# Causal attention that takes the query roots in its softmax's scale, and memory queries loaded in two halves of tokens

## The chip, the core and the metric

The kernel runs on one core of a Trainium2 chip. The metric is the device time of one execution in microseconds; three executions of the kernel before took 2182.63, 2183.37 and 2185.61 us, so the median is 2183.37.

In the profile the engines are PE (TensorE, matmuls and transposes), PEld (its weight loads), DVE (VectorE), ACT (ScalarE), POOL (GpSimd) and SP (SyncE, which issues all the loads and stores here). Each engine works its own instructions in order and waits on semaphores for the others.

## What is computed

One layer of a decoder trunk on 1024 tokens of width 1024 in float32: a half-step SwiGLU, a mixer with three gated branches, and another half-step SwiGLU. The change lies in the mixer. Cut to what matters:

```python
h = rmsnorm(x, mix_norm);  z = h @ w_in        # u | v | c_q | c_kv | k_rope | q_mem | gates
y_a = u * (tril(W_s) @ layernorm(v) + b)       # chunks of 128 tokens, 8 groups of 64
q = rmsnorm(q_up, q_norm)                      # c_q up to 8 heads of 96 (64 plain, 32 rotary)
q = concat(q[..., :64], rope(q[..., 64:]))     # k the same way, its rotary part shared
s = where(causal, (q @ k.T) * 96**-0.5, -1e30)
y_b = softmax(s) @ v                           # 8 heads, 1024 tokens
y_c = memory_attention(q_mem, mem)             # 4 heads of 128, 256 memory tokens
x = x + (sum_i sigmoid(gate_i) * (y_i @ W_branch_i)) @ W_out
```

The root of a query's RMSNorm is one number per token and head. A rotation works within a token and head, so such a factor may be applied before it, after it, or on the scores.

## The kernel before

**Products.** Float32 values are held as two parts, hi and lo, and a product is three matmuls, hi by hi, hi by lo, lo by hi (`mm3`, L156 to L163, matmuls at L160 to L162). `split` (L135 to L139) makes the parts: a cast on ACT (L136) and a difference on DVE (L139). `split_gain` (L151 to L154) does it with a gain per partition. PSUM gives two "mm" buffers of two banks each and four single "bank" buffers. A matmul row of 512 columns whose output is a bank, with operands named x and whi or wlo, is a branch product in the stretch that matters here.

**What sets the order.** A scheduler orders the instructions of each engine, from the order of the code and its own costs; `after(i, first)` (L414) holds an instruction behind another one of its engine. `self.hold` does so for every ACT cast of `split`, and for weight loads. SP issues all loads in its own order over eight rotating semaphores, so no more than eight transfers are in flight.

**qkv** (L440 to L503) works on pairs of token tiles, four passes. Queries and keys go up from their latents, ACT copies them out and squares them, DVE sums the squares, and an iterated reciprocal root gives r, 16 numbers per token tile pair and partition for q and 16 for k. DVE multiplies all of q by its roots (L490, 128x1536), POOL rotates q's rotary part (L369 to L374), DVE multiplies k (L492). The results go to DRAM: v (L478), k (`kd`, L495), q (`qd`, L498). The memory key and value weights (wkv, L808) are loaded in the same stretch.

**sgu** (L569 to L620) is the gated branch, in two halves of 512 tokens: `split(hf)` makes the parts of v, `mix(hf)` mixes tokens with eight group matrices, evicts with a bias on ACT (L591), transposes (L597), multiplies by u (loaded at L594), and splits. Between the halves lies `mem_kv` (L777 to L799), the memory's keys (split with a gain, L152 and L153) and values. Behind it the memory's queries are loaded (`mem_queries`, L814 to L822, issue L820): per head a hi and a lo tile of 128 features x 1024 tokens, 512 KB each. Heads 0 and 1 go to tiles named h, heads 2 and 3 to the tiles v_hi and v_lo of the first half, and those are issued first.

**Memory attention** (L824 to L881) follows a list written out by hand of S (scores of 128 tokens, 4 heads against 256 memory tokens, one mm buffer), T (transposes), V (values) and F. F is one step of branch a's output product, which fills PE in between; it loads a gate (L521) and multiplies on DVE (L1045). A score's chain is: DVE reduce (L838), DVE product with the roots of the memory queries (L839), four exps on ACT (L843, their scale one column of the negated roots), reciprocal (L847), normalisation on POOL (L848). The exps read the mm buffer, so the buffer is free when the fourth is done.

**Causal attention** (L889 to L1036) works head by head on pairs j of token tiles 2j and 2j+1, 32 steps. `prepare` transposes q and k of the next head and splits them with their gains. `scores` makes the scores of two tiles, one mm buffer each. For each, DVE adds the mask, writes the result to a tile pr and takes the minimum (L946; the gain has a minus sign, so the minimum is the maximum of the scores); ACT then takes the exps with that column as bias, scale -1, and a running sum (L952). `turn` transposes the exps in blocks (L968) into banks and splits them, `value` multiplies them with v (L983, L984) and evicts (L991, L992). The loop runs the turn one step and the value two steps behind the scores.

Of the kernel before, what the change touches and what calls it, by code (L numbers as in the profile page):

```python
# [8 lines left out]
F32 = mybir.dt.float32  # L9
# [3 lines left out]
ACT = mybir.ActivationFunctionType  # L13
# [3 lines left out]
P = 128  # L17
D = 1024
S = 1024
# [30 lines left out]
class Kernel:  # L50
# [84 lines left out]
    def split(self, hi, lo, src, eng=None):  # L135
        i = self.nc.scalar.copy(hi, src)  # L136
        if self.hold is not None:
            self.after(i, self.hold)
        return (eng or self.nc.vector).tensor_tensor(lo, src, hi.bitcast(F32), op=ALU.subtract)  # L139

    def split_after(self, hi, lo, src):
        i = self.nc.scalar.copy(hi, src)
        self.nc.vector.tensor_tensor(lo, src, hi.bitcast(F32), op=ALU.subtract)
        return i
# [294 lines left out]
    def qkv(self, lat, asides):  # L439
# [8 lines left out]
        with tc.tile_pool(name="qkvp", bufs=1) as p, tc.tile_pool(name="q1", bufs=1) as p1:  # L448
            for i0 in range(0, NT, 2):
                k = p.tile([P, T, H, QK], F32, name="k", bufs=2)  # L450
                q = (p1 if i0 % 4 else p).tile([P, T, H, QK], F32, name="q")
# [36 lines left out]
                bq = r[:, 0].unsqueeze(3)  # L488
                bk = r[:, 1].unsqueeze(3)
                nc.vector.tensor_tensor(q, q, bq.to_broadcast([P, T, H, QK]), op=ALU.mult)  # L490
                self.rotate(nc.gpsimd, q[:, :, :, NOPE:], q[:, :, :, NOPE:], tabs, [P, T, H, half])
                mark = nc.vector.tensor_tensor(k, k, bk.to_broadcast([P, T, H, QK]), op=ALU.mult)  # L492
                for t in range(T):
                    d = self.kd[:, :, i0 + t].rearrange("g p e -> p g e")
                    nc.sync.dma_start(d, k[:, t].rearrange("p (g x) d -> p g (x d)", x=2))  # L495
                for t in range(T):
                    d = self.qd[:, :, i0 + t].rearrange("g p e -> p g e")
                    self.queue = nc.sync.dma_start(d, q[:, t].rearrange("p (g x) d -> p g (x d)", x=2))  # L498
# [4 lines left out]
    def branches(self, br, yt, sink):  # L503

        nc, a, w = self.nc, self.a, {}

        steps = [(dt, hf) for hf in range(2) for dt in range(3)]
        steps += [(dt, hf) for dt in range(3, DT) for hf in range(2)]

        def weights(d):  # L510
            if d not in w:
                x = self.load(a["w_branch"][br, d // 2])
                w[d // 2 * 2], w[d // 2 * 2 + 1] = x[:4], x[4:]

        weights(0)
        yield
        for n, (dt, hf) in enumerate(steps):
            for d, _ in steps[n:n + 2]:
                weights(d)
            sig = self.row()  # L520
            nc.sync.dma_start(sig, self.sig[br * DT + dt][:, hf])  # L521
# [48 lines left out]
    def sgu(self, rows, p, sink):  # L570
        nc, a, tc = self.nc, self.a, self.tc
        v8 = lambda tag, hf, dt=F32R: (p if hf else self.pv).tile([P, 4, SGW], dt, name=tag)
        if True:
# [8 lines left out]
            def mix(hf):  # L582
# [4 lines left out]
                for g in range(SGG):  # L587
                    b = self.bank()[:, :4 * SGW // SGG].rearrange("p (c d) -> p c d", c=4)
                    cols = slice(g * SGW // SGG, (g + 1) * SGW // SGG)
                    self.mm3(b, w[g], tuple(x[:, :, cols] for x in v), True, True)  # L590
                    nc.scalar.activation(views[g // 4][:, :, g % 4], b, ACT.Identity, bias=self.sg_b[:, g:g + 1])  # L591
                for j in range(4):
# [6 lines left out]
                    i = self.split_after(*(t[:, hf * 512:hf * 512 + 512] for t in yt[j]), u)  # L599
                return i, z  # L600
# [8 lines left out]
            split(1)  # L609
            nc.scalar.activation(self.stat("warm", 1), vs[1][0][:, 3, SGW - 1:].bitcast(F32), ACT.Exp, scale=0.0)  # L610
# [4 lines left out]
            late = self.mem_queries(1, iter([tuple(x[:, i] for x in rooms) for i in range(2)]), z)  # L615
            queries = self.mem_queries(0, iter(lambda: self.split_pair(self.h4), None), z) + late
# [197 lines left out]
    def mem_queries(self, pair, rooms, first):  # L814

        out = []
        for o in range(2):
            qs = next(rooms)
            for t, src in zip(qs, self.mq[2 * pair + o]):
                self.after(self.nc.sync.dma_start(t.bitcast(F32), src), first)  # L820
            out.append(qs)
        return out  # L822

    def mem_attention(self, qt, rooms, kt, vv, filler):  # L824
# [5 lines left out]
        def scores(i, k):  # L830
            t = 2 * i + k
            sc = self.mm().rearrange("p a (b m) -> p (a b) m", b=2)
            for hh in range(MH):
                self.mm3(
                    sc[:, hh], tuple(x[:, t * P:(t + 1) * P] for x in qt[hh]), tuple(x[:, hh] for x in kt),
                    True, True)
            mx = self.stat("m_mx", MH)
# [34 lines left out]
        F = lambda: next(filler, None)  # L872
        yt = [self.split_pair(self.h4) for _ in range(MH)]
        for f, *x in (
                (F,), (F,), (S, 0, 0), (F,), (S, 0, 1), (F,), (F,), (T, 0, 0), (S, 1, 0), (F,), (T, 0, 1), (S, 1, 1),
# [13 lines left out]
    def attention(self):  # L889
# [15 lines left out]
        with tc.tile_pool(name="att", bufs=1) as p:  # L905
# [21 lines left out]
            def scores(h, j):  # L927
# [7 lines left out]
                for t in range(2):  # L935
# [14 lines left out]
                    prs.append(pr)  # L950
                for t, (pr, n) in enumerate(zip(prs, ns)):
                    nc.scalar.activation(  # L952
                        pr[:, :n], pr[:, :n], ACT.Exp, bias=mx[:, t:t + 1], scale=-1.0, accum_out=rs[:, t:t + 1])
# [1263 lines left out]
```

## Time and profile before

The profiled execution took 2181.75 us by the device; its span in the trace is 2180.0 us.

| What | Value |
|---|---|
| median of three runs | 2183.37 us |
| profiled execution, its span | 2181.75 us, 2180.0 us |
| mean granted TensorE clock | 0.999 |
| instructions | 27531 |
| read from and written to HBM | 229.33 MB, 109.84 MB |
| first loads of wkv behind qkv's third pass, issued | 1103.74 us |
| memory attention, first score | 1154.00 us |
| causal attention | about 1267 to 1410 us |

Times within the trace count from the span's start. A row of the timeline has the start, the time, the engine, the line of the code, the operation, output and inputs by the program's names with partitions x elements, and in brackets how long the engine had been idle before and who released it. A row of the waits has the total, the number of times and the longest. A row of the windows has the stretch and its length, busy time and (instructions) of PE, PEld, DVE, ACT and POOL, the granted clock, the busy share of the DMA engines and GB/s. A row of a line's view has the number of instructions, least, median and greatest nanoseconds, and the first and last start; a row of the groups has the number, the busy time in us and the mean in ns. A matmul of 512 columns is shown with 0.39 us but the next one starts 0.23 us later, since they are pipelined; one of 256 columns follows after 0.12.

### The profile page before, as it was taken

Reading aid. Unit: us, or ns where it says so; the run is one execution under the profiler, and the core shown is the slowest. Engines: PE = TensorE matmul, PEld = TensorE weight load, DVE = VectorE, ACT = ScalarE, POOL = GpSimd, SP = SyncE. Lnnn points to the kernel's source line nnn. Section 1 sums busy time; section 2 is a strip of 40 time slices with the busy share of each in tenths; the row PEclk is TensorE's granted clock in tenths of the full one; section 3 lists DMA queues with packets and bytes.
Section 4 is the critical chain, followed back from the end, with each engine's and each line's share of the span. In section 5 each row is a group of like instructions: output and inputs, shape, how many; then the busy total and the mean of one; then the engine's idle time right before and its main releaser. Section 6 shows DMA issues by size and latency. Waiting matters only on the chain.

```text
span 2180.0 us, 27531 instructions
## 1 busy us (share of the span) xinstructions
PE 2160.0 (99%) x10154; PEld 1802.9 (83%) x10154; DVE 1574.5 (72%) x2374; ACT 911.4 (42%) x1491; POOL 273.5 (13%) x278
## 2 busy tenths in 40 slices
PE   9999999999999999999999999999999999999999
PEld 5888888888887888888988889988888888888887
DVE  7976666679889656655895679885886666657884
ACT  5433333343445334433554368833432222224332
POOL 2011111100000000000232321140011211210000
PEclk9999999999999999999999999999999999999999
DMA  4264554385433444541685731093043233337443
GB/s 146 92 218 163 185 176 174 137 319 172 130 116 104 147 166 166 209 147 61 231 320 217 266 121 59 30 351 123 34 140 102 93 101 99 114 130 291 169 130 106
DMA packets 128823, 340.98 MB, mean 156 GB/s; under 512 B 15152, under 2 KB 23472, under 8 KB 128688
## 3 DMA queue, kind: packets, MB, share of 16 engines
q1 hardware_dynamic: 128688, 339.22, 44.5%
q8 instruction: 80, 1.31, 0.2%
q14 instruction: 55, 0.45, 0.1%
HBM read 229.33 MB, written 109.84 MB: 156 GB/s over the span
## 4 chain that ended last, share of the span: by engine, by line
PE 91%; DVE 5%; ACT 2%; issue 1%; DMA 1%; POOL 0%; SPq 0%; ACTq 0%; DVEq 0%; POOLq 0%
PE one L160 15%; PE one L161 15%; PE one L162 15%; PE bank L160 12%; PE bank L162 12%; PE bank L161 12%; PE mm L160 2%; PE mm L161 2%; PE mm L162 2%; PE bank L968 1%; PE bank L983 1%; PE bank L984 1%; PE bank L432 1%; DVE wlo L149 1%; DVE wlo L139 0%
## 5 line engine op out<-in xcount | busy, mean ns | idle before, releaser
L148 ACT CAST whi<-x 128x1024 fp32r<-128x1024 f32 (+1 forms) x203 | 193.2, 955 | 419.4 <-PE one L161 141.7
L149 DVE TENSOR_TENSOR wlo<-x,whi 128x1024 fp32r<-128x1024 f32 (+1 forms) x203 | 242.2, 1194 | 57.9 <-ACT whi L148 21.6
L1376 DVE TENSOR_TENSOR t<-t,one 128x512 f32<-128x512 f32 x188 | 129.0, 686 | 194.0 <-PE one L162 193.8
L160 PE MATMUL bank<-h,whi 128*128 128x512 f32 x636 | 247.6, 390 | 0.0
L162 PE MATMUL bank<-h,wlo 128*128 128x512 f32 x636 | 247.5, 389 | 0.0
L161 PE MATMUL bank<-h,whi 128*128 128x512 f32 x636 | 247.5, 389 | 0.0
L160 PE MATMUL one<-h,whi 128*128 128x512 f32 x516 | 202.3, 392 | 0.0
L161 PE MATMUL one<-h,whi 128*128 128x512 f32 x516 | 201.5, 391 | 0.0
L162 PE MATMUL one<-h,wlo 128*128 128x512 f32 x516 | 201.3, 390 | 0.0
L160 PE MATMUL one<-w,whi 128*128 128x512 f32 x432 | 168.6, 390 | 0.0
L162 PE MATMUL one<-w,wlo 128*128 128x512 f32 x432 | 168.1, 389 | 0.0
L161 PE MATMUL one<-w,whi 128*128 128x512 f32 x432 | 168.1, 389 | 0.0
L139 DVE TENSOR_TENSOR wlo<-w,whi 128x1024 fp32r<-128x1024 f32 (+2 forms) x112 | 114.7, 1038 | 70.1 <-ACT whi L136 69.9
L136 ACT CAST whi<-w 128x1024 fp32r<-128x1024 f32 (+2 forms) x112 | 99.0, 901 | 149.8 <-PE bank L161 53.7
L1958 POOL TENSOR_TENSOR raw<-raw 128x512 f32<-128x512 f32 x38 | 56.9, 1498 | 783.6 <-DVE raw L1813 684.8
L162 PEld LDWEIGHTS bank<-h,wlo 128*128 128x128 f32 x636 | 119.4, 188 | 24.9
L161 PEld LDWEIGHTS bank<-h,whi 128*128 128x128 f32 x636 | 119.4, 188 | 24.7
L160 PEld LDWEIGHTS bank<-h,whi 128*128 128x128 f32 x636 | 119.4, 188 | 24.6
L160 PE MATMUL bank<-whi 128*128 128x512 f32 x352 | 136.9, 389 | 0.0
L161 PE MATMUL bank<-wlo,whi 128*128 128x512 f32 x352 | 136.9, 389 | 0.0
L162 PE MATMUL bank<-whi,wlo 128*128 128x512 f32 x352 | 136.9, 389 | 0.0
L162 PEld LDWEIGHTS one<-h,wlo 128*128 128x128 f32 x516 | 97.3, 189 | 20.3
(391 smaller groups left out, 4913.2 us busy)
## 6 DMA issues: line engine op xcount, KB each, us to landing
x<-in_ffn_w_gu_dram SPq DMA_DIRECT2D x78, 512.0 KB, 4.9
w<-tdt SPq DMA_DIRECT2D x40, 512.0 KB, 4.5
gate<-raw SPq DMA_DIRECT2D x33, 512.0 KB, 2.9
tdb<-raw SPq DMA_DIRECT2D x64, 256.0 KB, 2.2
h<-in_ffn_w_down_dram SPq DMA_DIRECT2D x64, 256.0 KB, 6.0
w<-tdb SPq DMA_DIRECT2D x30, 512.0 KB, 4.4
tdt<-w SPq DMA_DIRECT2D x48, 256.0 KB, 2.3
x<-in_w_gate_dram SPq DMA_DIRECT2D x22, 512.0 KB, 7.1
```

Of the source, the lines that this page charges most:

```text
L136: i = self.nc.scalar.copy(hi, src)
L139: return (eng or self.nc.vector).tensor_tensor(lo, src, hi.bitcast(F32), op=ALU.subtract)
L148: self.nc.scalar.copy(hi, src)
L149: return lambda: self.nc.vector.tensor_tensor(lo, src, hi.bitcast(F32), op=ALU.subtract)
L160: i = mmul(out, s[0], m[0], start=first, stop=False, **kw)
L161: mmul(out, s[0], m[1], start=False, stop=False, **kw)
L162: self.last = mmul(out, s[1], m[0], start=False, stop=last, **kw)
L432: nc.tensor.transpose(b[:m, k * P:(k + 1) * P], s, self.ident)
L968: nc.tensor.transpose(b[:, at:at + P], prs[t][:, kk * P:(kk + 1) * P], self.ident)
L983: nc.tensor.matmul(o, w, pt[0], start=n == 0, stop=False)
L1376: return self.nc.vector.tensor_tensor(out, x, y, op=ALU.add)
L1958: sub = lambda d, x, y: (eng or nc.gpsimd).tensor_tensor(d, x, y, op=ALU.subtract)
```

## The change

1. In `qkv` the multiply of q by its roots goes (L490). POOL keeps the negated roots in a table `q_nr` (128 x 8 tiles x 8 heads), and q is rotated and written unscaled. Of the tile pools, q gets the two buffers that k had, and k takes q's arrangement. `self.queue`, behind which weight loads are held, is now the k write and no longer the q write.
2. In the causal attention a new DVE instruction per pair multiplies the two minima by -1 and the roots, and the exps take the root's column as scale. Both exps of a pair read that instruction's result.
3. `mem_queries` loads 512 tokens of all four heads per call, 256 KB a load, 16 loads. The first halves are held behind the last load of u as before; the second halves behind the gate load `sig_mark`, at a place Q in the list. Heads 0 and 1 are tiles named h as before, and are now issued in the order of the heads' list.
4. The first matmul of S(0,0) and S(0,1) is held behind the product before it (`after(first, last)`).
5. In `sgu` the split of v's second half runs inside `mix(0)`, held behind its last L591. The casts of branch a's weights are held behind the last cast of `mem_kv`.

```diff
     def split(self, hi, lo, src, eng=None):
-        i = self.nc.scalar.copy(hi, src)
+        self.cast = i = self.nc.scalar.copy(hi, src)
...
-                bq = r[:, 0].unsqueeze(3)
+                nc.gpsimd.tensor_scalar(self.q_nr[:, i0:i0 + T], r[:, 0], -1.0, None, op0=ALU.mult)
                 bk = r[:, 1].unsqueeze(3)
-                nc.vector.tensor_tensor(q, q, bq.to_broadcast([P, T, H, QK]), op=ALU.mult)
                 self.rotate(nc.gpsimd, q[:, :, :, NOPE:], q[:, :, :, NOPE:], tabs, [P, T, H, half])
...
+                if then:
+                    self.hold = i
+                    then()
+                    self.hold = None
...
-            mark, _ = mix(0)
-            kv = next(kv)
-            _, z = mix(1)
+            mix(0, second)
+            kv, mark = next(kv), self.cast
+            z = mix(1)
...
+    def mem_queries(self, qs, half, first):
+
+        c = slice(half * 512, half * 512 + 512)
+        for ts, src in zip(qs, self.mq):
+            for t, x in zip(ts, src):
+                self.after(self.nc.sync.dma_start(t[:, c].bitcast(F32), x[:, c]), first)
...
+                last = self.last
+                first = self.mm3(
                     sc[:, hh], tuple(x[:, t * P:(t + 1) * P] for x in qt[hh]), tuple(x[:, hh] for x in kt),
                     True, True)
+                if i == hh == 0:
+                    self.after(first, last)
...
-                (F,), (F,), (S, 0, 0), (F,), (S, 0, 1), (F,), (F,), (T, 0, 0), (S, 1, 0), (F,), (T, 0, 1), (S, 1, 1),
+                (F,), (F,), (Q,), (S, 0, 0), (F,), (S, 0, 1), (F,), (F,), (T, 0, 0), (S, 1, 0), (F,), (T, 0, 1), (S, 1, 1),
...
+                nr = self.q_nr[:, 2 * j:2 * j + 2, h]
+                nc.vector.scalar_tensor_tensor(mx, in0=mx, scalar=-1.0, in1=nr, op0=ALU.mult, op1=ALU.mult)
                 for t, (pr, n) in enumerate(zip(prs, ns)):
                     nc.scalar.activation(
-                        pr[:, :n], pr[:, :n], ACT.Exp, bias=mx[:, t:t + 1], scale=-1.0, accum_out=rs[:, t:t + 1])
+                        pr[:, :n], pr[:, :n], ACT.Exp, bias=mx[:, t:t + 1], scale=nr[:, t:t + 1],
+                        accum_out=rs[:, t:t + 1])
```

Three places show what moves. The first is PE at the beginning of the memory scores; mm is a score's buffer (the number tells S(0,0)'s from S(0,1)'s), h4 in front of the comma the memory keys, behind it the queries of heads 0 and 1, and bank the product of branch a. Before:

```order
L160 MATMUL bank_9408<-x4_9034,whi_9283 128x512
L160 MATMUL mm_9341<-h4_9002,h4_9273 128x256
L161 MATMUL mm_9341<-h4_9003,h4_9273 128x256
L160 MATMUL mm_9382<-h4_9002,h4_9273 128x256
L161 MATMUL mm_9382<-h4_9003,h4_9273 128x256
L161 MATMUL bank_9408<-x4_9035,whi_9283 128x512
L162 MATMUL bank_9408<-x4_9034,wlo_9284 128x512
L160 MATMUL bank_9408<-x4_9036,whi_9283 128x512
L162 MATMUL mm_9341<-h4_9002,h4_9274 128x256
L162 MATMUL mm_9382<-h4_9002,h4_9274 128x256
```

And now, with `mm3` five lines lower:

```order
L156 MATMUL bank_9376<-x4_9024,whi_9319 128x512
L155 MATMUL mm_9350<-h4_9003,h4_9270 128x256
L156 MATMUL mm_9350<-h4_9004,h4_9270 128x256
L157 MATMUL bank_9376<-x4_9023,wlo_9320 128x512
L157 MATMUL mm_9350<-h4_9003,h4_9271 128x256
L155 MATMUL bank_9376<-x4_9025,whi_9319 128x512
L156 MATMUL bank_9376<-x4_9026,whi_9319 128x512
L155 MATMUL mm_9350<-h4_9003,h4_9272 128x256
L156 MATMUL mm_9350<-h4_9004,h4_9272 128x256
L157 MATMUL bank_9376<-x4_9025,wlo_9320 128x512
L155 MATMUL bank_9376<-x4_9027,whi_9319 128x512
L157 MATMUL mm_9350<-h4_9003,h4_9273 128x256
```

Before, two mm buffers take turns, and S(0,0) and S(0,1) stay interleaved to the end of both; five branch matmuls follow, and then S(1,0) begins. Now S(0,0) has its buffer to itself: its four heads follow with five branch matmuls among them, five more branch matmuls stand behind it, then the 12 of S(0,1) without anything between, then 24 of the branch, and then S(1,0). Of branch a, 43 matmuls stand ahead of the first score before and 26 now. The fourth of the query tiles, h4_9273 now, is first read ten rows behind the first score.

The second is SP at the loads of the memory queries (mq), from the last of the v tiles' loads. Before:

```order
L820 DMA v_lo_9268<-mq_3366 128x1024
L521 DMA t_9299<-gate0_3332 128x512
L521 DMA t_9324<-gate1_3333 128x512
L820 DMA h4_9273<-mq_3366 128x1024
L820 DMA h4_9274<-mq_3366 128x1024
L820 DMA h4_9277<-mq_3366 128x1024
L820 DMA h4_9278<-mq_3366 128x1024
```

And now, from the last two loads of the v tiles:

```order
L822 DMA v_hi_9268<-mq_3366 128x512
L822 DMA v_lo_9269<-mq_3366 128x512
L100 DMA raw_9829<-in_w_branch_dram 128x1024
L822 DMA h4_9270<-mq_3366 128x512
L822 DMA h4_9271<-mq_3366 128x512
L822 DMA h4_9272<-mq_3366 128x512
L822 DMA h4_9273<-mq_3366 128x512
```

Before, four whole v loads and two gate loads stand ahead of the four h loads. Now four first halves of the v tiles come first, then the two gate loads, then the four second halves (the last two are shown) and one branch weight load, then the four first halves of h, and behind them the four second halves.

The third is ACT at the last two pairs of the causal attention (tiles pr of 640 to 1024 columns). Before:

```order
L952 ACTIVATE pr5_12332,a_rs_11948<-pr5_12332,a_mx_12315 128x768
L991 COPY ysum_12268<-bank_12255 64x256
L952 ACTIVATE pr6_12368,a_rs_11948<-pr6_12368,a_mx_12360 128x896
L136 CAST whi_12286<-bank_12288 128x384
L952 ACTIVATE pr7_12377,a_rs_11948<-pr7_12377,a_mx_12360 128x1024
L991 COPY ysum_12268<-bank_12296 64x256
L136 CAST whi_12336<-bank_12338 128x512
```

And now:

```order
L136 CAST whi_12325<-bank_12327 128x384
L958 ACTIVATE pr4_12362,a_rs_11981<-pr4_12362,a_mx_12354,q_nr_8322 128x640
L958 ACTIVATE pr5_12371,a_rs_11981<-pr5_12371,a_mx_12354,q_nr_8322 128x768
L958 ACTIVATE pr6_12408,a_rs_11981<-pr6_12408,a_mx_12400,q_nr_8322 128x896
L998 COPY ysum_12306<-bank_12335 64x256
L958 ACTIVATE pr7_12417,a_rs_11981<-pr7_12417,a_mx_12400,q_nr_8322 128x1024
L136 CAST whi_12376<-bank_12378 128x512
```

The exps of a pair stand next to each other or nearly so, and what stood between them, a cast of 128x384, is ahead of them. The cast of 128x512 that both have behind the last exp serves the turns of tiles 2 and 3.

More of the change, by code (lines that the diff above doesn't have):

```diff
@@ L520, in branches @@
             sig = self.row()
-            nc.sync.dma_start(sig, self.sig[br * DT + dt][:, hf])
+            self.sig_mark = nc.sync.dma_start(sig, self.sig[br * DT + dt][:, hf])
             b = self.bank()
@@ L580, in split, with mix @@
                     self.v_mark = self.split(*(x[:, 2 * i:2 * i + 2] for x in vs[hf]), v)
-            def mix(hf):
+            def mix(hf, then=None):
                 if not yt:
```

41 lines of the change are left out of this document (16 added, 25 removed).

## The prediction

> **What bounds the kernel now.** I read the page first: the busy times and the chain that ended last.
>
> ```profile
> PE 2160.0 (99%) x10154; PEld 1802.9 (83%) x10154; DVE 1574.5 (72%) x2374; ACT 911.4 (42%) x1491; POOL 273.5 (13%) x278
> PE 91%; DVE 5%; ACT 2%; issue 1%; DMA 1%; POOL 0%; SPq 0%; ACTq 0%; DVEq 0%; POOLq 0%
> ```
>
> TensorE issues matmuls nearly all the time, and the change takes away none of them. So it can only move the few microseconds in which TensorE stands, and work taken from another engine is worth nothing unless TensorE waits for it. The waits of PE, the second view, show where that happens; these are the rows that fall in the stages the change touches.
>
> ```profile
> PE mm L160 <- ACT v_hi L843: 4.0, 2, 3.5
> PE bank L160 <- DVE h L153: 1.7, 2, 1.1
> PE mm L160 <- DVE a_mx L946: 1.0, 1, 1.0
> PE bank L160 <- ACT h L591: 0.8, 1, 0.8
> ```
>
> The first is the memory scores (L834), the second and fourth the gating mix, the third the start of the causal attention. Third, the table by stage: qkv up to 1130, the second gating mix, the branch beside the memory queries' loads, the first memory scores, the start of attention, the rest of it.
>
> ```profile
> 1105.00:1130.00 25.00, 25.00 (x124) 21.27 (x123) 24.19 (x62) 10.07 (x23) 13.08 (x12) 1.00 1.01 366
> 1130.00:1145.00 15.00, 12.44 (x84) 10.74 (x83) 14.57 (x22) 13.48 (x25) 0.00 (x0) 1.00 0.98 366
> 1145.00:1155.00 10.00, 10.00 (x48) 8.33 (x47) 4.36 (x7) 1.24 (x3) 0.00 (x0) 1.00 1.03 408
> 1160.00:1170.00 10.00, 5.99 (x41) 5.04 (x40) 5.60 (x11) 5.57 (x20) 3.75 (x2) 1.00 0.66 230
> 1267.00:1300.00 33.00, 31.85 (x229) 29.23 (x228) 29.10 (x68) 28.72 (x65) 4.43 (x15) 1.00 0.19 65
> 1300.00:1410.00 110.00, 109.36 (x810) 101.94 (x809) 98.73 (x218) 98.05 (x222) 21.17 (x69) 1.00 0.08 30
> ```
>
> PE is full in the qkv row and in the row of the loads; it misses 2.6 us in the mix, 4.0 at the memory scores and 1.15 + 0.64 in attention. DMA is at its limit from 1105 to 1155, and in attention DVE and ACT are both near 90%.
>
> **The change part by part.** The sum is made against the profiled execution, 2181.75 us (span 2180.0), which lies 1.6 under the median of 2183.37; I add that back at the end.
>
> *Query roots out of qkv.* Four DVE multiplies go.
>
> ```profile
> L490 DVE TENSOR_TENSOR q<-q,rs_y x4: 1757/1759/2182, 1081.9 to 1118.2; 128x1536 f32<-128x1536 f32 x4
> POOL t L369 <- DVE q L490: 34.3, 4, 18.4
> ```
>
> That is 3 x 1.76 + 2.18 = 7.5 us of DVE, but PE stood for nothing in this stage, so the gain is 0, and cannot be more. The four new POOL copies of the roots are 128x16, ahead of the rotation that no longer waits for L490. What moves is SP: the q writes become ready sooner and stand ahead of other loads in SP's order. The fourth pass's writes (tokens 3) now come before the wkv loads, which began at 1103.74, and the rotation would end about 0 to 1.8 us after that. The wkv loads start the stretch in which DMA is full, so such a delay reaches the query loads whole; it is counted there.
>
> *The mix.* The second half's split of v now waits for the last L591 of the first half, where it stood before anyway, and the casts of the branch weights are released after mem_kv's last cast instead of after the first mix. On ACT four weight casts come ahead of the second mix's L591 in place of two, and the k pair L152/L153 stands together. The 1.7 + 0.8 us stays, by less than one L136 cast either way: 0, bounds -0.6 and +0.6.
>
> *Query loads in halves.* The timeline of the first memory scores, on PE, DVE and ACT:
>
> ```profile
> 1159.51 0.28 PE L162 MATMUL mm<-h,v_lo 128*128 128x256 f32 x1
> 1160.56 0.40 PE L162 MATMUL bank<-x,wlo 128*128 128x512 f32 x1
> 1164.47 0.38 PE L160 MATMUL mm<-h,h 128*128 128x256 f32 x1 [3.52 <-ACT v_hi L843]
> 1158.99 2.35 DVE L838 TENSOR_REDUCE m_mx<-mm 128x4 f32<-128x1024 f32 x2 [8.40 <-PE mm L162]
> 1161.85 0.16 DVE L839 TENSOR_TENSOR m_mx<-m_mx,mq_r 128x4 f32<-128x4 f32 x1
> 1162.13 0.56 ACT L843 ACTIVATE v_hi<-mm,m_mx,mq_nr 128x256 f32<-128x256 f32 x1 [15.89 <-DVE m_mx L839]
> ```
>
> S(0,0) and S(0,1) are woven together and end together at 1159.5. Both mm buffers are then full, five branch matmuls are left, and S(1,0) needs a buffer whose four exps end at 1164.4. Afterwards S(0,0) stands whole, S(0,1) behind it, and 24 branch matmuls before S(1,0). From the end of S(0,0) to S(1,0) PE has 12 small and 29 large matmuls, 12 x 0.12 + 29 x 0.23 = 8.1 us. The chain that frees the buffer is a reduce of 1.2 (half of 2.35), 0.16, and four exps whose starts lie 0.55 apart: 3.6 us, about 4.2 with the hops between engines. It is covered twice over: **-4.0**.
>
> What is late next is the data. S(0,0) starts 17 branch matmuls earlier (26 of them stand ahead of it instead of 43):
>
> ```profile
> 1154.00 0.28 PE L160 MATMUL mm<-h,h 128*128 128x256 f32 x1
> L820 SPq DMA_DIRECT2D h<-mq x4: 319/320/358, 1140.5 to 1145.0; - x4
> DMA to landing us min/median/max: 6.7/9.0/10.4
> GB/s 382 328 455 328 382 437 382 346 437 382 401 419 401 382 437 346 346 364 273 219 146 73 73 91 73 55 55 18 18 36 18 36 18 18 36 18 36 18 18 0
> ```
>
> Before, the last of the h loads was issued at 1145.0 and, 9.0 later, landed at 1154.0, just as PE reached it. Now PE comes at 1154.0 - 17 x 0.23 = 1150.1, and needs the fourth h tile some 1.8 us later, 1151.9. The halves do less than they seem to: the second halves of the v tiles and a weight load are issued ahead of the first halves of h, so 4.0 MB lead up to S(0,0) instead of 4.5. At the 408 GB/s of the 1145 to 1155 row, 0.5 MB is 1.3 us: the last half tile lands at about 1152.8, and PE waits 0.9. Bounds: 0, and with the 1.8 us of the wkv loads 2.7. I take **+0.9**, since the q write's delay is most likely near zero. The last row is the rate in slices of 0.11 us from 1157; from the ninth slice only 256 KB loads were left, and they moved about 390 GB/s in the ten slices before they ran out, so pieces of half the size cost 4% at most, 0.4 us over these 4 MB, inside the bounds.
>
> [...]
>
> The later scores and turns also change places, S(3,1) coming last; PE lost little there before, and I take +0.2 (-0.3 to +1.0).
>
> *Attention.* Each of the 32 pairs gets a DVE product of 128x2 and exps whose scale is a column. The nearest rows:
>
> ```profile
> L839 DVE TENSOR_TENSOR m_mx<-m_mx,mq_r x8: 149/156/854, 1161.9 to 1196.0; 128x4 f32<-128x4 f32 x8
> L843 ACT ACTIVATE v_hi<-mm,m_mx,mq_nr x16: 553/569/597, 1162.1 to 1189.6; 128x256 f32<-128x256 f32 x16
> L952 ACT ACTIVATE pr<-pr,a_mx 128x256 f32<-128x256 f32 x8 | 4.1, 511 | 0.0
> L136 ACT CAST whi<-bank 128x512 fp32r<-128x512 f32 x48 | 26.5, 579 | 0.2
> L152 ACT ACTIVATE h<-bank,a_gq 96x512 fp32r<-96x512 f32 x16 | 10.9, 679 | 0.2
> ```
>
> DVE: 32 x 0.156 = 5.0 us. ACT: a column as scale costs 0.569 - 0.511 = 0.06 by the exps (though one source is another memory) or 0.679 - 0.579 = 0.10 by L152 against the cast, so 64 times that, 3.7 to 6.4 us; the exps are nearer. The stage of 143 us holds 127.8 of DVE and 126.8 of ACT, so both still fit and the load alone costs nothing.
>
> [...]
>
> What can cost is the chain. Before, the exp of a pair's first tile ran while DVE reduced the second; now both wait for both reduces and the product, and they stand on ACT ahead of the casts of other turns. At the end of the stage nothing covers this; ACT, DVE and PE there:
>
> ```profile
> 1398.66 1.05 ACT L952 ACTIVATE pr<-pr,a_mx 128x896 f32<-128x896 f32 x1
> 1400.97 1.15 ACT L952 ACTIVATE pr<-pr,a_mx 128x1024 f32<-128x1024 f32 x1 [0.40 <-DVE a_mx L946]
> 1402.63 0.97 ACT L136 CAST whi<-bank 128x512 fp32r<-128x512 f32 x2
> 1399.70 1.22 DVE L946 CUSTOM_DVE_ANT_0 pr<-mm,mask 128x1024 f32<-128x1024 f32 x1 [0.58 <-PE mm L162]
> 1404.00 1.01 PE L968 MATMUL bank<-ident,pr 128*128 128x128 f32 x7 [0.23 <-DVE wlo L139]
> ```
>
> The last exp began when its reduce was done, and the casts at 1402.63 free the banks for which PE stands at 1404.00. In the new order both last exps follow that reduce and the casts follow them, so the casts come later by the product, the exp of 896 and the dearer scales, 0.16 + 1.05 + 0.12 = 1.3: **+1.3** (0.3 to 2.0). In the middle heads of the new order PE has 10 to 13 us of matmuls (counted row by row at the rates above) between the last row of a score and its first turn, in the first and last head 3.3 to 7.7 at the tightest places, against a longest chain of 1.22 + 0.16 + 1.05 + 1.15 = 3.6 us, 3.9 with hops, and 1.5 for the pair at the 3.3. The turns are covered; the casts that stand behind the exps on ACT are the doubt: **+1.0** (-0.6 to +4.0), the lower end being a third of the 1.8 us that PE lost in the stage, the upper an eighth of the lateness worked out for the second rival.
>
> Sum: -4.0 + 0 + 0.9 + 0.2 + 1.3 + 1.0 = -0.6. That gives 2181.15 for such an execution and **2182.8** on the median's footing. A measurement of this kernel can tell about 0.2%, 4.4 us, from no change; the forecast is no change.
>
> **The rivals.** *Attention swallows it all (faster).* The casts are late nowhere that PE waits, the tail is hidden too, and the loads come in time: -4.0 - 0.6 (mix) - 0.3 (later scores) = -4.9, so 2178.5. For it: the 10 us between score and turn. Against: the tail's rows, and that it needs the mix's term to pass 4.4.
>
> *The exp pairs become the wait (slower).* Per head the first exps (1.05 for 896, 0.51 for 256, by size about 0.8 and 0.65 between) move behind the second reduce: some 3.0 us, with four products 0.6 and eight dearer exps 0.5, 4.1 us a head and 33 over eight heads. The place is ACT: the casts of the turns wait behind exps that wait for DVE, the banks stay full, and PE stands at the next transpose. It decides when a cast is late by more than PE's work up to the next bank that it needs. If a quarter of the 33 shows, 8.2 takes the place of 1.3 + 1.0: -4.0 + 0.9 + 0.2 + 8.2 = +5.3, 2188.7. For it: both engines at 90%, in order. Against: PE lost only 1.8 us here before.
>
> *The queries come late (about the same).* The wkv loads slip by 1.8, the halves run at a lower rate, and S(0,0) waits for both, 0.9 + 1.8 + 1.3 = 4.0, the last term what the halves gained: -4.0 + 4.0 + 0.2 + 1.3 + 1.0 = +2.5, 2185.9. The halves then do not do what they say. For it: DMA at 1.01 and 1.03; against: the 390 GB/s above. [...]
>
> **How the numbers follow.** Forecast 0.48, swallowed 0.28, exp pairs 0.15, late queries 0.09. Of the forecast a twentieth each way passes 4.4, and of the swallowed case a tenth stays inside: faster 0.28, slower 0.17, the rest, 0.55, within. The likeliest case alone spans 2179.5 to 2186.5; the range takes in the swallowed case with the 1.5 us by which single runs differ, and ends at the exp pairs' figure, 2177.0 to 2188.7.
>
> **What would show it.** Right: the L843 wait of 4.0 gone; the first memory scores at about 1150 to 1151 instead of 1154, with PE waiting for a DMA of mq there by about 1 us; DVE lighter by 7.5 us before 1130 with no change on PE; L956 at 0.15 to 0.16 us, exps longer by 0.06 to 0.1; a PE wait of one to two microseconds at the end of attention. Wrong: PE waits for the exps or the wlo of the turns repeated from head to head, a DMA wait of 3 us or more before the memory scores, or a stall in the mix that grew past 4 us.

## The result and the profile after

The changed kernel takes 2198.45 us (median of four, 2197.84 to 2199.24) against 2184.47 for the kernel before in the same comparison: 14 us slower, a ratio of 1.0065 (95% interval 1.0048 to 1.0082). The forecast was 2182.8 with no measurable change, and its range ended at 2188.7. The forecast was wrong.

The profiled execution took 2197.84 us, its span is 2196.1, so 16.1 us more than the profiled execution before. Three marks in the trace divide them. The first transpose of a query in the causal attention starts at 1265.3 instead of 1267.4: 2.1 us gained up to there. The last transpose of an exp starts at 1424.2 instead of 1407.9: the attention stage takes 158.9 us instead of 140.5, 18.4 lost. Behind it nothing changes, within 0.2. So all of the loss is in attention, and it is larger than the result.

From the page, the busy times, with about 7 us more on PE though it has the same 10154 instructions:

```profile
PE 2166.9 (99%) x10154; PEld 1808.8 (82%) x10154; DVE 1573.3 (72%) x2402; ACT 920.0 (42%) x1491; POOL 272.8 (12%) x282
```

The waits of PE, those of the stages of the change:

```profile
PE bank L975 <- ACT t L1012: 6.4, 3, 2.1
PE bank L990 <- DVE ysum L999: 3.5, 3, 1.5
PE bank L975 <- DVE wlo L139: 2.5, 2, 1.5
PE bank L155 <- ACT h L586: 2.1, 1, 2.1
PE mm L155 <- DVE a_mx L950: 1.0, 1, 1.0
PE bank L155 <- DVE h L148: 0.6, 1, 0.6
```

The wait of the memory scores for the exps (4.0 us) is gone. The three new ones at the top are all in attention, and all are for PSUM banks: PE wants to transpose (L975) or to multiply by v (L990), and the bank that it needs has not been read out by ACT (L1012, the copy of the softmax's reciprocals) or DVE (L999, the addition of the value's other half, and L139, the difference of a split). The same stages as before, in the table by window:

```profile
1105.00:1130.00 25.00, 25.00 (x127) 21.58 (x126) 18.65 (x59) 9.13 (x22) 6.41 (x8) 1.00 1.01 366
1130.00:1145.00 15.00, 12.24 (x72) 10.61 (x71) 12.20 (x17) 13.03 (x24) 0.00 (x0) 0.94 0.90 311
1145.00:1155.00 10.00, 10.00 (x53) 8.78 (x52) 6.36 (x10) 2.96 (x5) 0.00 (x0) 0.92 1.04 380
1160.00:1170.00 10.00, 10.00 (x60) 8.73 (x59) 7.73 (x14) 6.26 (x19) 3.79 (x2) 1.00 0.78 267
1267.00:1300.00 33.00, 30.24 (x209) 26.83 (x208) 27.96 (x72) 27.94 (x61) 3.42 (x16) 1.00 0.19 65
1300.00:1410.00 110.00, 100.64 (x712) 94.39 (x709) 90.48 (x218) 89.87 (x196) 17.88 (x57) 0.95 0.08 30
```

Two columns matter. PE is idle for 9.4 us of the last row, where it was idle for 0.6; and the granted clock, 1.00 in all of these rows before, is 0.95 there and 0.92 to 0.94 around the memory queries. DVE and ACT are *less* busy in the last row than before (90.5 and 89.9 us of 110 against 98.7 and 98.1), so neither was overloaded. It is an order in which each waits for the other.

One of the places where that happens, a head's pair of 896 and 1024 columns, on DVE, ACT and PE in turn:

```profile
1311.11 1.23 DVE L950 CUSTOM_DVE_ANT_0 pr<-mm,mask 128x1024 f32<-128x1024 f32 x1 [0.28 <-PE mm L157]
1312.83 0.75 DVE L148 SCALAR_TENSOR_TENSOR h<-bank,g_ev_k,h 96x512 fp32r<-96x512 f32 x1
1313.50 0.15 DVE L956 SCALAR_TENSOR_TENSOR a_mx<-a_mx,q_nr 128x2 f32<-128x2 f32 x1
...
1316.55 0.42 DVE L999 TENSOR_TENSOR ysum<-ysum,bank 64x256 f32<-64x256 f32 x1 [2.44 <-ACT ysum L998]
...
1313.68 1.14 ACT L958 ACTIVATE pr<-pr,a_mx,q_nr 128x896 f32<-128x896 f32 x1 [1.08 <-DVE a_mx L956]
1314.81 1.22 ACT L958 ACTIVATE pr<-pr,a_mx,q_nr 128x1024 f32<-128x1024 f32 x1
1316.15 0.36 ACT L998 COPY ysum<-bank 64x256 f32<-64x256 f32 x1
1316.54 0.59 ACT L1012 COPY t<-bank 128x512 f32<-128x512 f32 x1
...
1314.46 0.60 PE L975 MATMUL bank<-ident,pr 128*128 128x128 f32 x4
1317.18 0.90 PE L975 MATMUL bank<-ident,pr 128*128 128x128 f32 x3 [2.12 <-ACT t L1012]
1318.73 0.41 PE L155 MATMUL mm<-h,h 96*128 96x256 f32 x1
```

The kernel before at the same pair, both exps, the second reduce and the same copy:

```profile
1309.00 1.06 ACT L952 ACTIVATE pr<-pr,a_mx 128x896 f32<-128x896 f32 x1
1309.70 1.22 DVE L946 CUSTOM_DVE_ANT_0 pr<-mm,mask 128x1024 f32<-128x1024 f32 x1
1311.71 1.16 ACT L952 ACTIVATE pr<-pr,a_mx 128x1024 f32<-128x1024 f32 x1
1313.44 0.59 ACT L1005 COPY t<-bank 128x512 f32<-128x512 f32 x1
```

Read the first block from the bottom up. PE stands from 1315 to 1317.18 for a bank that the copy L1012 frees. The copy is short, but on ACT it stands behind the two exps, and those stand behind the DVE product, for which ACT idled 1.08 us. The product in its turn stands on DVE behind the reduce of the second tile, a ysum addition and a key's difference. DVE then idles 2.44 us for ACT's ysum copy, which is also behind the exps. Before, the exp of 896 columns had run beside the second reduce, and the copy began 2.6 us after that reduce; now it begins 4.3 us after it.

PE's idle time in the whole attention stage is 14.1 us, against 1.5 before: 158.93 - 144.84 and 140.57 - 139.12 in these two windows, before and now.

```profile
1267.36:1407.93 140.57, 139.12 (x1021) 129.31 (x1020) 125.52 (x282) 124.70 (x281) 24.84 (x83) 1.00 0.11 39
1265.29:1424.22 158.93, 144.84 (x1021) 133.93 (x1020) 129.75 (x314) 130.81 (x281) 25.46 (x83) 0.97 0.10 34
```

The other part is the clock. The last PE row of the pair above starts its successor 0.21 us later, where one of 256 columns took 0.12. The same stretch and the two like it as windows:

```profile
1317.50:1320.50 3.00, 3.00 (x16) 2.97 (x15) 2.13 (x4) 1.99 (x5) 1.68 (x5) 0.50 0.03 8
1358.50:1361.50 3.00, 3.00 (x16) 2.97 (x15) 2.13 (x4) 1.86 (x6) 1.49 (x5) 0.50 0.00 0
1399.50:1402.50 3.00, 3.00 (x16) 2.97 (x15) 2.17 (x5) 1.96 (x5) 1.26 (x5) 0.50 0.00 0
```

The clock is granted at exactly half for 3.4 us, by half-microsecond windows, each time behind a gap of 2.39 us from one start to the next. A stretch costs at most 3.4 x 0.5 = 1.7 us, three at most 5.1. Together 12.6 + 5.1 = 17.7 of the 18.4 us of the stage; the rest is not traced. In the 3.4 us ahead of each stretch PE idled 2.1.

### The profile page after: what moved, and what is told of

Its sections match the earlier page's. It is cut to its first block, busy times and chain, and to the rows that moved or that the text cites. A ratio compares the mean times of both kernels' runs of the same rounds, so it can differ in the third digit from the quotient of the medians.

```text
span 2196.1 us, 27538 instructions
## 1 busy us (share of the span) xinstructions
PE 2166.9 (99%) x10154; PEld 1808.8 (82%) x10154; DVE 1573.3 (72%) x2402; ACT 920.0 (42%) x1491; POOL 272.8 (12%) x282
## 4 chain that ended last, share of the span: by engine, by line
PE 91%; DVE 5%; ACT 3%; issue 1%; POOL 0%; DMA 0%; SPq 0%; ACTq 0%; POOLq 0%; DVEq 0%
PE one L155 15%; PE one L156 15%; PE one L157 15%; PE bank L155 12%; PE bank L156 12%; PE bank L157 12%; PE mm L155 2%; PE mm L156 2%; PE mm L157 2%; PE bank L975 1%; ACT pr L958 1%; PE bank L990 1%; DVE wlo L144 1%; PE bank L991 1%; PE bank L427 1%
## 5 line engine op out<-in xcount | busy, mean ns | idle before, releaser
L139 DVE TENSOR_TENSOR wlo<-w,whi 128x1024 fp32r<-128x1024 f32 (+2 forms) x112 | 114.7, 1037 | 68.5 <-ACT whi L136 68.3
L156 PEld LDWEIGHTS one<-h,whi 128*128 128x128 f32 x516 | 97.3, 189 | 20.3 <-issue 0.2
```

The source lines that it names most:

```text
L156: mmul(out, s[0], m[1], start=False, stop=False, **kw)
```

## The experiments

Theory A is what the trace shows: the exps of a pair, tied together by the product, hold up on ACT the copies and casts that free PE's banks. Theory B puts the loss on the exps' longer time with a column as scale, theory C on the other parts (halves, mix, the clock behind them). Ratios are to runs of the kernel before on the same chip. The versions ran on several chips, on which the kernel before took 2183.95 to 2185.13 us, so a difference between two versions is good to about a microsecond. The scheduler orders every version anew, so a run shows what an edit costs together with the order that the scheduler then writes.

**The halves alone.** The multiply L490 and the exps of before are put back into the changed kernel.

```diff
-                nc.vector.scalar_tensor_tensor(mx, in0=mx, scalar=-1.0, in1=nr, op0=ALU.mult, op1=ALU.mult)
...
-                        pr[:, :n], pr[:, :n], ACT.Exp, bias=mx[:, t:t + 1], scale=nr[:, t:t + 1],
+                        pr[:, :n], pr[:, :n], ACT.Exp, bias=mx[:, t:t + 1], scale=-1.0, accum_out=rs[:, t:t + 1])
```

> The changed kernel with the query roots back in qkv and the old exps, so the halves and the new order of the mix alone. Theory A (the exps of a pair, back to back on ACT behind the DVE product, hold up the copies and casts that free PE's banks) and theory B (the column as scale makes ACT too slow): attention as before, the start of attention 2 us earlier as in the changed kernel, so about 2182.5 us (2180 to 2184), 2 us under before. Theory C (the loss comes from the halves, the mix and the lower clock behind them): 2195 or more.

Measured: 2178.78 us against 2184.67, ratio 0.9971 (0.9959 to 0.9983). Faster, by 5.9 us rather than 2 (4.6 between the two profiles). PE's waits from 1100 to 1420 in this kernel:

```profile
PE bank L155 <- DVE h L148: 1.7, 2, 1.1
PE mm L155 <- DVE a_mx L950: 1.0, 1, 1.0
PE bank L987 <- DVE wlo L139: 0.3, 1, 0.3
```

And its long window of attention:

```profile
1300.00:1410.00 110.00, 109.35 (x811) 102.03 (x810) 98.79 (x215) 98.20 (x218) 21.18 (x69) 1.00 0.10 36
```

Attention is that of before to 0.1 us (140.6 from mark to mark). Theory C falls. The 4 us of the memory scores are won, and the gap of 2.1 us that the changed kernel has in the mix (below) is not here: it needs the roots, too.

**The roots alone**, the whole of parts 1 and 2 of the change on the kernel before.

> The kernel before with the roots in the softmax's scale alone, no halves, the old mix. A and B: the attention stage costs the 18 us that it cost in the changed kernel and nothing is gained ahead of it, about 2202 us (2199 to 2204). C: near before, 2187 at most.

Measured: 2204.77 us, ratio 1.0087 (1.0072 to 1.0102), 20.1 us slower. The waits at the top are the same three, 6.4, 3.5 and 2.5 us; the attention stage took 161.8 us in its profile, with two more half-rate stretches in it than the changed kernel has. The measured time lies just above the expected 2204. Halves and roots add up: -5.9 + 20.1 = 14.2, against the 14.0 of the whole change.

**The pair without the column.**

```diff
+            minus = p.tile([P, 2], F32, name="minus")
+            nc.gpsimd.memset(minus, -1.0)
...
+                nc.vector.scalar_tensor_tensor(mx, in0=mx, scalar=-1.0, in1=minus, op0=ALU.mult, op1=ALU.mult)
```

> The kernel before with one more DVE product per pair, by a constant tile of -1 and by -1, ahead of both exps; the scale stays the constant -1. So the pair waits as in the change, and the exps cost what they did. A: PE waits for banks at the pairs of 896 and 1024 columns, 8 to 16 us slower than before (2192 to 2200). B: at most 1 us slower.

Measured: 2196.72 us, ratio 1.0054 (1.0037 to 1.0071), 12 us slower. The exps cost what they did (1136 ns at 1024 columns against 1156), so theory B cannot explain it. PE waits for the same banks:

```profile
PE bank L971 <- ACT t L1008: 2.3, 3, 1.5
PE bank L971 <- DVE wlo L139: 2.3, 1, 2.3
...
PE bank L986 <- DVE ysum L995: 1.4, 1, 1.4
```

**The column without the pair**, read from the same tile of -1.

```diff
-                        pr[:, :n], pr[:, :n], ACT.Exp, bias=mx[:, t:t + 1], scale=-1.0, accum_out=rs[:, t:t + 1])
+                        pr[:, :n], pr[:, :n], ACT.Exp, bias=mx[:, t:t + 1], scale=minus[:, t:t + 1], accum_out=rs[:, t:t + 1])
```

> The kernel before with the exps' scale read from a constant tile of -1, and no product; the order on every engine is that of before. Each exp should take 0.075 to 0.1 us more, 5.4 us of ACT in the stage. A: within 2 us of before (2183 to 2187). B: 10 us slower or more, PE waiting for exps or casts.

Measured: 2185.07 us, ratio 1.0001 (0.9992 to 1.0011). The exps of 256 and 1024 columns in this kernel, then those of the changed one and its product:

```profile
L954 ACT ACTIVATE pr<-pr,a_mx,minus 128x256 f32<-128x256 f32 x8 | 4.8, 603 | 0.0
L954 ACT ACTIVATE pr<-pr,a_mx,minus 128x1024 f32<-128x1024 f32 x8 | 10.0, 1245 | 0.9 <-DVE a_mx L948 0.9
```

```profile
L958 ACT ACTIVATE pr<-pr,a_mx,q_nr 128x256 f32<-128x256 f32 x8 | 4.7, 590 | 0.0
L958 ACT ACTIVATE pr<-pr,a_mx,q_nr 128x1024 f32<-128x1024 f32 x8 | 9.8, 1231 | 0.0
L956 DVE SCALAR_TENSOR_TENSOR a_mx<-a_mx,q_nr 128x2 f32<-128x2 f32 x32 | 4.9, 152 | 0.4
```

Against 511 and 1156 before, the column costs 0.075 to 0.09 us an exp, some 5.4 us of ACT in the stage, and the kernel does not feel it. ACT's order in attention is that of before but for five exps, each one place earlier. Theory B falls as the cause by itself.

**Pair and column together**, with the multiply of q left in qkv; the edit is that of the last two.

> The kernel before with the product per pair by a constant tile of -1 and the scale read from that tile, so pair and column together; the multiply of q by its roots stays in qkv. ACT's order in attention is that of the changed kernel. If the part of the change in qkv is innocent: as much slower as the roots alone, 2202 to 2206 us. If pair and column only add up (12 and 0.4): 2197, and the rest of the 20 us comes from qkv.

Measured: 2200.27 us, ratio 1.0072 (1.0057 to 1.0087), 15.9 us slower. That lies between the two expectations. Pair and column do more together than 12 + 0.4: ACT's order is now nearly that of the changed kernel, with the gaps of 2.39 us, three half-rate stretches and 158.0 us from mark to mark. The roots alone are another 4.5 us slower. Their profile is 6.5 longer: 3.8 of it in attention, where it has two more half-rate stretches, and 2.9 ahead of attention, where it has one more and PE waits 0.9 us in qkv against 0.2 here.

**One product per tile**, right behind its reduce, in the changed kernel.

```diff
+                    one = self.q_nr[:, i, h:h + 1]
+                    nc.vector.scalar_tensor_tensor(
+                        mx[:, t:t + 1], in0=mx[:, t:t + 1], scalar=-1.0, in1=one, op0=ALU.mult, op1=ALU.mult)
...
-                nc.vector.scalar_tensor_tensor(mx, in0=mx, scalar=-1.0, in1=nr, op0=ALU.mult, op1=ALU.mult)
```

> The changed kernel with a product of 128x1 per tile right behind its reduce, in place of one of 128x2 per pair. The exp of a pair's first tile no longer waits for the second reduce; the exps still stand next to each other on ACT, ahead of the same copies and casts. If the wait of the first exp is what holds ACT up: ACT can take it in the time in which it stood for the product, and the loss in attention shrinks to a quarter or less, 2180 to 2186 us. If the place of the two exps on ACT alone does it: at most 3 us better than the changed kernel, 2195 or more.

Measured: 2187.09 us, ratio 1.0013 (1.0003 to 1.0022). Of the 19.7 us between the changed kernel and the halves alone, 11.4 come back, more than half but not three quarters; the time lies in neither of the two expected ranges. ACT and DVE at the pair that was shown above, in this kernel:

```profile
1309.87 1.14 ACT L960 ACTIVATE pr<-pr,a_mx,q_nr 128x896 f32<-128x896 f32 x1
1311.01 0.67 ACT L147 ACTIVATE h<-bank,g_ev_k 96x512 fp32r<-96x512 f32 x1
1312.14 1.25 ACT L960 ACTIVATE pr<-pr,a_mx,q_nr 128x1024 f32<-128x1024 f32 x1
1313.50 0.37 ACT L1000 COPY ysum<-bank 64x256 f32<-64x256 f32 x1
...
1311.95 0.16 DVE L954 SCALAR_TENSOR_TENSOR a_mx<-a_mx,q_nr 128x1 f32<-128x1 f32 x1
```

The exp of 896 columns again runs beside the reduce of the other tile, and the ysum copy starts 2.1 us after the second reduce ends instead of 3.9 (1313.50 and 1316.15, against 1311.4 and 1312.3). No stretch of attention has half clock: it is 1.00 in every half-microsecond window from 1200 to 1500. What is left are shorter waits for the same banks, and a stage of 147.3 us.

**A product per tile only in the pairs of 896 and 1024 columns**, one per pair elsewhere.

> The changed kernel with a product per tile only in the pairs of 896 and 1024 columns, and one per pair elsewhere. If these eight pairs carry the loss, as PE's gaps say: nearly as good as a product per tile everywhere, 2185 to 2190 us. If the loss lies in all pairs: three quarters of it stay, 2193 or more.

Measured: 2189.57 us, ratio 1.0018 (1.0008 to 1.0027). These eight pairs give back 8.9 of the 11.4 us, so most of the loss lies in them.

**A product per tile without the column**, on the halves alone, by a tile of -1.

> The halves alone (old qkv, constant scale) with a product of 128x1 per tile by a constant tile of -1 behind each reduce: the per-tile products without the column as scale. It stands between the halves alone (2178.8) and the per-tile products with the column (2187.1). If the product behind each reduce, in the way of the exp, is what is left: 2184 to 2187. If the column's 0.08 us per exp is what is left, now that the exps stand in the way: 2179 to 2182.

Measured: 2184.51 us, ratio 0.9997 (0.9987 to 1.0006). Of the 8.3 us that stay with a product per tile, 5.7 are here without any column. The two profiles say where the rest is: attention takes 146.9 us here and 147.3 with the column, so that the column costs 0.4 there, and the other 2.1 lie ahead of attention, where this version has the old qkv. The products cost the 6.3 us of the stage through the order on ACT that comes with them (the exps of 896 and 1024 columns next to each other, ahead of the copies) or through their own hops between engines; these two were not separated.

**The product on POOL**, as two instructions, so that nothing of DVE stands ahead of it.

```diff
-                nc.vector.scalar_tensor_tensor(mx, in0=mx, scalar=-1.0, in1=nr, op0=ALU.mult, op1=ALU.mult)
+                nc.gpsimd.tensor_tensor(mx, mx, nr, op=ALU.mult)
+                nc.gpsimd.tensor_scalar(mx, mx, -1.0, None, op0=ALU.mult)
```

> The changed kernel with the pair's product on POOL, as two instructions of 128x2 (by the negated roots, then by -1), so that it no longer stands on DVE behind a ysum eviction and a key's difference, which delayed it by 1.2 us behind the last reduce in the pairs of 896 and 1024 columns. Both exps still wait for both reduces and stand on ACT in the same order. If that delay on DVE is a main part of the loss: 8 heads by up to 1.2 us and fewer half-rate stretches, 2186 to 2192 us. If the pairing alone does it: 2195 to 2200, and more if POOL's two instructions and hops take longer than the 1.2 us.

Measured: 2195.07 us, ratio 1.0049 (1.0032 to 1.0066): 3.4 us better than the changed kernel, at the edge of the second expectation. POOL had the second product at 1312.71 and ACT began the exp of 896 columns at 1313.40, 0.3 us sooner than in the changed kernel (1313.68). PE still waited 4.0 us for L1013 (the copy of the reciprocals) and 4.6 for L1000 (the ysum addition). But the run did not take the delay away: from the end of the second reduce to the exp it is still 1.1 us instead of 1.4. Nor did it keep ACT's order, as had been expected: at this pair a ysum copy now stands ahead of both exps. So it does not show how much of the loss the delay on DVE makes.

**The exps held behind the copies.** The exps are written behind the turn and value of the earlier steps, and those of 896 and 1024 columns are held on ACT behind the last copy of the value two steps back.

> The changed kernel with the exps written behind the turn and value of the earlier steps, and those of 896 and 1024 columns held on ACT behind the last copy of the value two steps back (the ysum copy, or the copy of the reciprocals). The product per pair stays. Theory A: the waits for the copy and for the ysum eviction, 9.9 us in the changed kernel, go, and 2.39 us gaps with them; 2184 to 2192 us, unless the exps now come too late for their own turns. If the order on ACT does not matter: 2197 to 2200, as the changed kernel.

Measured: 2211.86 us, ratio 1.0122 (1.0101 to 1.0143), the slowest of all. The wait for the copy is indeed gone, but the scheduler now puts exps and reduces of the next head ahead, and PE stands at the value products instead:

```profile
PE bank L996 <- DVE wlo L139: 8.6, 5, 2.0
PE bank L996 <- DVE a_mx L961: 6.4, 3, 2.2
```

So neither expectation came true: the bank wait was moved to another instruction, not removed. The run shows that the place of the exps matters, and no better place.

**The halves with the old mix.** Part 5 of the change is undone as well.

> The halves alone, with the old order of the mix and the old attention. If the halves carry the gain of 5.9 us and the new order of the mix about 1 us of it (a gap of 1.06 us behind the biases): 2179.5 to 2181. If the new order of the mix carries more, 2182 or more; if it costs, under 2178.

Measured: 2178.13 us, ratio 0.9968 (0.9956 to 0.998), 6.3 us faster, in neither of the expected ranges. The new order of the mix gives nothing that can be measured. What gains are parts 3 and 4 of the change, the loads in halves and the hold on the first scores; no run separates these two. This version and the halves alone are the ones that beat both kernels.

## Why the prediction was wrong

**Attention (+1.3 and +1.0 forecast, +18.4 measured)** is the step that failed: the term for the copies and casts that stand behind the exps on ACT, which the sum had at +1.0 and bounded at +4.0. The prediction had the mechanism, as the rival on the slower side: "the casts of the turns wait behind exps that wait for DVE, the banks stay full, and PE stands at the next transpose". It gave it 0.15 and 8.2 us, on the ground that a quarter of 33 us of lateness would show, and preferred the case in which "the turns are covered". The turns were covered: PE had 10 us of work between a score and its turn, and no wait of PE is for an exp. But that counted PE's instructions only up to the turn of the same pair. The copies that stand behind the exps on ACT serve the turn and the value of *earlier* pairs, for which PE has nothing in reserve, and PE uses all four banks. Of the new waits 9.9 us are for the copies of the reciprocals and the additions of the value, and only 2.5 for a split of the turns, which is what the rival named. The question to ask was not when the exp is needed, but who is queued behind it.

The prediction also looked at the load of DVE and ACT, about 127 of 143 us each, and found that both still fit. That was right, and did not help: neither became fuller; the waits arise because each stands for the other in order.

**The clock** was not in the sum at all. Three stretches of half rate are up to 5.1 us of the 18.4 in this profile, and the idle time of PE 12.6. The runs with a product per tile have no such stretch in the stage; the last section says why.

**The tail** (+1.3) is part of the same: the last head's gaps, from one start to the next, were 0.74 and 1.74 us before its turns and 0.63 before its values.

**The column** was costed at 3.7 to 6.4 us of ACT without effect; it is 5.4, and has none alone (2185.07 against 2184.67). **The product** at 0.156 us measured 0.152.

**The memory scores** (-4.0) were right. S(1,0) starts without a gap behind its branch matmul; the first exps are done long before:

```profile
1157.64 0.56 ACT L846 ACTIVATE v_hi<-mm,m_mx,mq_nr 128x256 f32<-128x256 f32 x1 [7.17 <-DVE m_mx L842]
...
1163.74 0.39 PE L157 MATMUL bank<-x,wlo 128*128 128x512 f32 x1
1163.96 0.28 PE L155 MATMUL mm<-h,h 128*128 128x256 f32 x1
```

**The wait for the loads** (+0.9, and the rival of late queries) did not come: PE has no wait for a DMA there. The fourth half tile landed at 1153.7, where 1152.8 had been reckoned, and PE itself reached the scores at 1153.3 instead of 1150.1, since the waits in qkv, the mix and the half-rate stretch behind it had put it back by some 3 us. That there was no wait is luck: a PE on time would probably have stood for the first half tile of h, which landed at 1151.7. The loads of the changed kernel:

```profile
L822 SPq DMA_DIRECT2D h<-mq x8: 319/320/1302, 1144.5 to 1151.0; - x8
...
DMA to landing us min/median/max: 4.8/6.0/7.2
```

They landed one every 0.67 us, half of the 1.28 of the whole tiles, so the size costs about a twentieth. The lower rate that the rival gave the halves was no more than that here, with DMA kept full (a busy share of 1.04 from 1145 to 1155).

**The mix** (0, within 0.6) was wrong in kind. The gaps add up to the same, but four weight casts stand ahead of the biases in one piece:

```profile
1142.53 0.39 PE L155 MATMUL bank<-v_hi,x 128*128 128x256 f32 x1 [2.08 <-ACT h L586]
...
1139.90 2.19 ACT L136 CAST whi<-raw 128x512 fp32r<-128x512 f32 x4
1141.99 2.90 ACT L586 ACTIVATE h<-bank,c_sg_b 128x256 f32<-128x256 f32 x7
```

One gap of 2.1 us in place of three shorter ones was followed by a half-rate stretch, 1143.1 to 1146.5, up to another 1.7 us. But the halves alone show such a stretch there too (clock 0.89 from 1130 to 1145), without this gap, so it is not the gap's alone, and it does not explain why 2.1 us were gained ahead of attention and not 4: the halves alone gained 4.2 with it. The 2.1 us between the two are about half in qkv and half in the longer gap of the mix.

**qkv** (0) was right in that the work taken from DVE gained nothing: 5.5 us less of it from 1105 to 1130 leave PE at 25.00 of 25.00. But the new order there cost a little. Between 1050 and 1105 PE was busy 54.16 of 55.00 us, with waits of 0.5 for a weight load and 0.4 for a split; before it was full.

## What to carry to other kernels

When an instruction is made to wait for one thing more, list what stands behind it on its engine and whose buffers that frees; the consumer of its own result may have plenty of time while the others have none. Tying two instructions to one small product that needs both inputs costs the overlap of the first with the second input; here 0.15 us of work, per tile instead of per pair, gave 11 us back. An engine that works in order can be the bound without being full: ACT was busy for 89.9 of 110 us.

## What the runs showed of the hardware

TensorE's granted clock fell to 0.50 for 3.4 us at a time. The roots alone, whose waits in attention are those of the changed kernel, have two such stretches more there (mean clock of the whole profile 0.994 against 0.996) and take 2.9 us longer in the stage, 161.8 against 158.9, so one costs about 1.5 us by this estimate, and 1.7 at most.

The length of a gap does not settle whether a stretch follows. In the changed kernel a gap of 2.39 us was followed by one three times of three, but the gap of 3.9 us before the memory scores in the kernel before was not (clock 1.00 in 1160 to 1170).

What agrees better with the traces is how the idle time lies against the stretches of the same profile. In the changed kernel the stretches begin at 1143.11, 1317.19, 1358.15 and 1399.11 and have 3.413 us each; from one to the next it is 174.08, 40.96 and 40.96 us, which is 51, 12 and 12 such lengths. With pair and column together they begin at 1139.44, 1320.35, 1361.31 and 1402.27, 53, 12 and 12 lengths apart, and with the product on POOL at 1142.68 and 1415.75, 80 lengths apart.

The idle time of PE was added up in steps of this length, counted from a profile's own stretches, in the kernel before, the changed one, the pair without the column, pair and column together, the product on POOL, the halves with the old mix, and a product per tile without the column and in the last pairs only. Between 1100 and 1430 (in the pair without the column from 1200) these eight profiles have nine steps at full clock in which PE idled for 1.9 us or more, and half clock followed all nine. It followed five of the nine steps with 1.7 to 1.9 us, among them one with 1.73 and not the one with 1.88, and none of the others, which had 1.53 at most. Each gap of 2.39 us put its idle time, 2.11 to 2.12 us, into one step. The gap of 3.9 us was cut into 1.80 and 1.72. Three of three is also less than it looks, for these gaps follow each other by 40.8 us, nearly 12 steps: where one lies within a step, the next do too. In the three versions with a product per tile PE idled for no more than 1.5 us in any 3.41 us from 1262 to 1430, and no stretch began there.

So in these profiles it depended on where the gaps fell on the steps whether a stretch, at up to 1.7 us, came behind them. Executions of one kernel differ in their clock too: four of the version with the exps held took from 2205.87 us at a mean clock of 0.997 to 2214.95 at 0.992. Whether the steps make this difference was not shown.
